# The second block's ssm input gathered with masked copies and matmuls, and the glu weight splits queued behind the last scan

## The chip, the cores and the metric

One core of a Trainium2 chip runs the whole program. The metric is the device time of one launch in microseconds (us). Engines are TensorE (PE; its weight loads are listed as PEld), VectorE (DVE), ScalarE (ACT), GpSimd (POOL) and SyncE (SP), which issues most transfers. Each engine runs its own instructions in order and waits on semaphores for the others.

## The reference, cut to what matters

The program is a trunk of two layers on a sequence of 256 steps with 1024 channels. Each layer is: half a SwiGLU feed-forward, a mixer, another half feed-forward, and a gated embedding, each with a normalization before and after. The first mixer is a differential attention, the second an S5 state-space layer followed by a GELU and a gated linear unit (glu). The change lies in the second mixer:

```
h = rmsnorm(x, g[2])
u = h in chunks, 64 groups of 16 channels, 64 complex states a group
state[t] = a * state[t-1] + B u[t]          (per group, complex, diagonal)
y[t] = Re(C state[t]) + d * u[t]
z = gelu(y) @ w_glu + b_glu
m = z[:, :1024] * sigmoid(z[:, 1024:])
```

## The kernel before, in words

The 256 steps are two blocks of 128 rows (b = 0, 1), held as x0 and x1 with a row per partition. Two generators (thread(0), thread(1)) walk the stages and share each weight tile; block 0 leads. Large matmuls are done in three passes: a weight tile is loaded raw by SP, ACT rounds it to a high part hi (line 129), VectorE subtracts to get the low part lo (line 131), and mm3 (lines 301 to 303) multiplies hi, lo and hi again. There are three raw buffers, so a new load waits until the lo of an earlier tile is done.

A planner orders the instructions of all engines from a model of their durations, except within ssm_core: there TensorE, VectorE and ACT keep the written order among the instructions of that function; instructions from outside it may still be put between them.

The ssm layer is computed by blocks of eight steps. Its input must be laid out so that a partition holds (step within eight, channel of the group) and the columns count groups and blocks of eight. ssm_u(b) (line 978) does the first half: as soon as a block's x is final, eight transfers per block copy x inside the on-chip memory into the tile ssmA, step s to slice s; those of block 0 go over SP's queue, those of block 1 over ACT's (six) and POOL's (two). ACT then squares the block (junku, line 1001), POOL makes the norm factor r, VectorE multiplies a 0/1 pattern with it (oh, line 1003). In ssm_core the order is: the embedding projection of both blocks (proj, 24 matmuls ppproj), two small matmuls that spread the norm factors (r_ps, line 1022), eight scaled copies ssmA to A2 (lines 1028 and 1030), then four gathers (lines 1050 to 1054: four transposes u_ps and one copy into ush each), mixed with the rest:

- chunk_states(pr): the states that each eight steps add, for a quarter of the groups (s_ps); needs the quarter of ush.
- turned(pr): transposes of them (st_ps). rotate(pr) and scan(pr) on VectorE: a rotation, two scans, a rotation back (lines 1092 to 1104); they give X.
- products(pr), outputs(pr): accumulate the direct part from ush and the part from X into y_ps. gated(hf): GELU on ACT, transposes y_tr, split into yT.
- glu_tile(n): lets one more glu weight tile be split (hi, lo); four such calls stand in the list. Other pending splits become free to go only after W.split_limit is raised at the end of ssm_core.

The glu matmuls (zglu) follow; the first 24 of each block need only the first half of yT and the first four weight tiles.

Of the kernel before, what the change touches and what calls it, by code (L numbers as in the profile page):

```python
# [140 lines left out]
def trunk(ctx, tc, x, p, norm_g, ffn_w_in, ffn_w_out, attn_w_qkv, attn_w_o, attn_lam, attn_subln_g,  # L141
# [835 lines left out]

    def ssm_u(b):

        if "A" not in ssm:  # L980
            gr = big_pool.tile([P, 640], F32, tag="hT_lo0", name="ssm_sel")
            ssm["R"], ssm["one"] = gr[:, 256:264], gr[:, 264:272]
            ssm["oh"], blk16 = [gr[:, 272:280], gr[:, 280:288]], gr[:, 288:304]
            ssm["sel"] = [gr[:, 320:448], gr[:, 448:576]]
            nc.vector.tensor_reduce(ssm["one"], ident.rearrange("p (j s) -> p s j", s=8), AX.X, ALU.add)
            nc.vector.tensor_reduce(blk16, ident.rearrange("p (j s) -> p j s", s=8), AX.X, ALU.add)
            for j in range(2):
                nc.gpsimd.memset(ssm["sel"][j], 0.0)
                nc.gpsimd.tensor_copy(ssm["sel"][j][:, 64 * j:64 * j + 64].rearrange("p (k q) -> p k q", q=4),
                                      blk16.rearrange("p (k o) -> p k o", o=1).broadcast_to([P, 16, 4]))  # L990
            ssm["A"] = big_pool.tile([P, 8, 256], F32, tag="hT_hi0", name="ssmA")
        xb = xs[b]
        steps_of = xb.rearrange("(k s) c -> s k c", s=8)
# [5 lines left out]
        junk = act_pool.tile([P, D], BF16, tag=f"xT_hi{b}", name=f"junku{b}")  # L999
        ss = small.tile([P, 1], F32, tag="ss", name=f"ssu{b}")  # L1000
        nc.scalar.activation(junk, xb, AF.Square, scale=1.0 / 32, accum_out=ss)
        r = rsqrt_of([ss], EPS, f"u{b}")
        nc.vector.tensor_scalar(ssm["oh"][b], ssm["one"], r, None, ALU.mult)
# [6 lines left out]
    def ssm_core(pool, pj, vs, tos, glu, heads):  # L1010

        A, v = ssm["A"], nc.vector
        W.split_limit = glu[0][0]
        both = [proj(b, 1, pj, heads[b]) for b in range(2)]
        for b in (0, 0, 0, 1, 1, 1):
            next(both[b], None)
        ush_xf = big_pool.tile([P, 2560], F32, tag="hT_hi1", name="ush")
        ush = ush_xf[:, :2048].rearrange("p (g t) -> p g t", t=P)
        A2 = big_pool.tile([P, 16, 8, 16], F32, tag="hT_lo1", name="ssmA2")
        rp = bank("a0", "r_ps")  # L1020
        for b in range(2):
            nc.tensor.matmul(rp[:, 0:8], ssm["sel"][b], ssm["oh"][b], start=b == 0, stop=b == 1)
        v.tensor_copy(ssm["R"], rp[:, 0:8])
        for s_ in range(8):
            dst = A2[:, :, 7 - s_, :]
            src = A[:, s_, :].rearrange("p (g h) -> p g h", h=16)
            if s_ % 3 == 2:
                nc.scalar.activation(dst, src, AF.Copy, scale=ssm["R"][:, s_:s_ + 1])
            else:
                v.tensor_scalar(dst, src, ssm["R"][:, s_:s_ + 1], None, ALU.mult)  # L1030
        S_xf = big_pool.tile([P, 2560], F32, tag="hT_lo0", name="ssmS")
        S = S_xf[:, :2048].rearrange("p (g r e n) -> p g r e n", g=8, r=2, e=2)
        xfs = [t[:, 2048:2560].rearrange("p (r c j) -> p r c j", r=2, j=32) for t in (S_xf, ush_xf)]
        yg = big_pool.tile([P, 2, 8, 8, 16], F32, tag="hT_hi0", name="ssmY")
        yT = [(act_pool.tile([P, KT, P], F32R, tag=f"xT_hi{b}", name=f"yThi{b}"),
               act_pool.tile([P, KT, P], F32R, tag=f"xT_lo{b}", name=f"yTlo{b}")) for b in range(2)]
        ssm["yT"] = yT
# [12 lines left out]
        def gather(g4, eng):  # L1050
            pt = ps_tr.tile([P, 512], F32, tag="tr", name=f"u_ps{g4}")
            for j in range(4):
                nc.tensor.transpose(pt[:, j * P:(j + 1) * P], A2[:, 4 * g4 + j].rearrange("p s h -> p (s h)"), ident)
            eng(ush[:, 4 * g4:4 * g4 + 4, :].rearrange("p a t -> p (a t)"), pt)

        def u_of(G):
            return ush[:, G].rearrange("p (m q) -> p q m", q=4)

        def chunk_states(pr):
            vv = ssm["V", pr] if pr < 2 else take2(vs[pr - 2])  # L1060
            for gg in range(2):
                gp = 2 * pr + gg
                acc = bank(f"a{gg}", f"s_ps{gp}")
                for e in range(2):
                    grouped(acc[:, e * P:(e + 1) * P], u_of(2 * gp + e), vv[gg][:, e * 512:e * 512 + 512],
                            start=True, stop=True)
                nc.scalar.copy(S[:, gp].rearrange("p r e n -> p e r n"),
                               acc[:, :2 * P].rearrange("p (e r n) -> p e r n", e=2, r=2))
# [9 lines left out]
        def rotate(pr):  # L1078
            er, rh = (ssm[k][:, 2 * pr:2 * pr + 2].rearrange("p g q j -> p (g q j)") for k in ("er", "rh"))
            er2 = er.rearrange("p (o x) -> p o x", o=1).broadcast_to([P, 2, 256])  # L1080
            eis = ssm["eis"][:, :, 2 * pr:2 * pr + 2].rearrange("p r g q j -> p r (g q j)")
            if pr % 2:
                r4 = big_pool.tile([P, 4, 2, 256], F32, tag="hT_lo1", name=f"rt{pr}")
# [12 lines left out]
        def scan(pr):  # L1096
# [7 lines left out]
            v.tensor_tensor(xf[:, :, :, 1:32], t1v[:, :, :, 0:31], t2v[:, :, :, 0:31], ALU.add)  # L1104
            X.append(xf.rearrange("p r c j -> p r (c j)"))

        def products(pr):
# [5 lines left out]
            for gg in range(2):  # L1113
                tt, to = take2(tos[2 * pr + gg])
                c0 = (2 * (pr % 2) + gg) * P
                for e in range(2):
                    grouped(accs_y[hf][e][:, c0:c0 + P], u_of(4 * pr + 2 * gg + e), tt[:, e * 512:e * 512 + 512],
# [32 lines left out]
        gather(0, nc.scalar.copy)  # L1150
        gather(1, v.tensor_copy)
        chunk_states(0)
        gather(2, nc.scalar.copy)
# [12 lines left out]
        scan(1)  # L1166
        turned(3)
# [12 lines left out]
        scan(3)  # L1180
# [3 lines left out]
        W.split_limit = len(specs)  # L1184

# [166 lines left out]
```

## Time and profile before

| | us |
|---|---|
| median of 3 runs (lowest, highest) | 1135.49 (1134.68, 1136.91) |
| the profiled execution, its own time | 1136.68 |
| its span, first to last instruction | 1134.9 |
| PE busy, share of the span | 1050.2, 93% |
| DVE busy, share | 690.1, 61% |
| ACT busy, share | 552.9, 49% |
| mean granted clock of TensorE (1 is full) | 0.967 |

A busy time sums an engine's instructions; overlapping ones count once. The ssm stage lies at about 811 to 880 us. In a list in order of time, a row gives the start, the length, the engine, the line, the operation, what it writes and reads, and how many alike it merges; in brackets how long the engine was idle before it and which instruction ended the wait. Two levels of TensorE's clock occur: 1.2 GHz (0.50) and 2.4 GHz (1.00).

### The profile page before, as it was taken

What the parts mean: (1) busy time and instruction counts of PE and PEld (TensorE: products, weight loads), DVE (VectorE), ACT (ScalarE), POOL (GpSimd) and SP (SyncE); (2) the same over time, 40 slices, a digit from 0 to 9 for tenths busy, and PEclk for the clock granted to TensorE, in tenths of its full rate; (3) what the DMA queues carried; (4) which work ended last, traced back from release to release, by engine and by line L of the source; (5) the groups of instructions that cost most, each with busy time, mean ns of one, the idle gap of its engine ahead of it and who ended that gap; (6) DMA issues with size and microseconds to landing.
All of it is one profiled execution on the core that took longest, in us unless ns stands there. A gap on an engine that the chain in (4) does not pass through costs nothing. (4 is left out here: it accounts for less than half of the span.)

```text
span 1134.9 us, 14522 instructions
## 1 busy us (share of the span) xinstructions
PE 1050.2 (93%) x5251; PEld 841.1 (74%) x5251; DVE 690.1 (61%) x1003; ACT 552.9 (49%) x872; POOL 241.7 (21%) x297
## 2 busy tenths in 40 slices
PE   6899999999998999998787998999776999999997
PEld 4688888788776887776565776888654878888885
DVE  6555554679558896555567563654357586555464
ACT  5544444566655544433464542553244475444354
POOL 6000000000020017878779412000100010000001
PEclk9899999999999999999898999999986999999999
DMA  7766556567447768566555669756874457665651
GB/s 225 225 185 186 185 189 193 161 201 219 146 96 192 222 187 219 187 203 211 161 169 165 182 176 335 237 178 220 285 256 149 154 164 231 183 193 163 210 168 56
DMA packets 119016, 217.58 MB, mean 192 GB/s; under 512 B 24832, under 2 KB 43168, under 8 KB 118944
## 3 DMA queue, kind: packets, MB, share of 16 engines
q1 hardware_dynamic: 115520, 210.14, 59.8%
q0 software_dynamic: 1888, 5.47, 2.0%
q10 hardware_dynamic: 1536, 1.05, 0.3%
q8 instruction: 41, 0.67, 0.3%
q14 instruction: 31, 0.25, 0.1%
HBM read 204.08 MB, written 15.69 MB: 194 GB/s over the span
## 5 line engine op out<-in xcount | busy, mean ns | idle before, releaser
L131 DVE TENSOR_TENSOR lo<-raw,hi 128x1024 fp32r<-128x1024 f32 x332 | 428.4, 1296 | 269.2 <-ACT hi L129 266.3
L129 ACT CAST hi<-raw 128x1024 fp32r<-128x1024 f32 x332 | 347.6, 1052 | 346.0 <-PE up L303 107.9
L301 PE MATMUL up<-hi,xThi 128*128 128x512 f32 x704 | 279.9, 401 | 13.0 <-ACT xThi L320 5.6
L302 PE MATMUL up<-lo,xThi 128*128 128x512 f32 x704 | 279.3, 398 | 2.1 <-DVE lo L131 2.0
L303 PE MATMUL up<-hi,xTlo 128*128 128x512 f32 x704 | 280.6, 404 | 0.0
L301 PEld LDWEIGHTS up<-hi,xThi 128*128 128x128 f32 x704 | 134.7, 192 | 42.3 <-ACT xThi L320 7.3
L302 PEld LDWEIGHTS up<-lo,xThi 128*128 128x128 f32 x704 | 134.7, 191 | 32.5 <-DVE lo L131 4.7
L303 PEld LDWEIGHTS up<-hi,xTlo 128*128 128x128 f32 x704 | 134.3, 192 | 29.1 <-issue 0.6
L301 PE MATMUL dn<-hi,hThi 128*128 128x512 f32 x352 | 139.9, 398 | 0.0
L302 PE MATMUL dn<-lo,hThi 128*128 128x512 f32 x352 | 139.0, 395 | 0.0
L303 PE MATMUL dn<-hi,hTlo 128*128 128x512 f32 x352 | 138.5, 394 | 0.0
L301 PEld LDWEIGHTS dn<-hi,hThi 128*128 128x128 f32 x352 | 67.0, 190 | 14.5 <-issue 0.8
L303 PEld LDWEIGHTS dn<-hi,hTlo 128*128 128x128 f32 x352 | 67.1, 191 | 14.2
L302 PEld LDWEIGHTS dn<-lo,hThi 128*128 128x128 f32 x352 | 67.1, 191 | 13.6
L312 POOL TENSOR_SCALAR v_pn<-sspn,sspn 128x1 f32<-128x1 f32 x8 | 3.4, 422 | 344.1 <-ACT junkpn L369 341.7
L320 ACT ACTIVATE xThi<-xT_ps,gT 128x128 fp32r<-128x128 f32 x112 | 38.6, 367 | 47.1 <-PE xT_ps L338 46.7
L325 DVE TENSOR_TENSOR hTlo<-hT_ps,hThi 128x512 fp32r<-128x512 f32 (+1 forms) x48 | 30.8, 644 | 40.3 <-ACT hThi L324 40.2
L324 ACT CAST hThi<-hT_ps 128x512 fp32r<-128x512 f32 (+1 forms) x48 | 26.4, 550 | 57.9 <-PE hT_ps L448 57.8
L321 DVE SCALAR_TENSOR_TENSOR xTlo<-xT_ps,gT,xThi 128x128 fp32r<-128x128 f32 x112 | 36.4, 345 | 23.8 <-ACT xThi L320 23.4
L338 PE MATMUL xT_ps<-ident,x 128*128 128x128 f32 x112 | 30.7, 298 | 16.0 <-DVE xTlo L321 11.1
L445 DVE SCALAR_TENSOR_TENSOR h<-up,r_pre,sg 128x512 f32<-128x512 f32 (+1 forms) x48 | 33.7, 702 | 15.7 <-ACT sg L443 10.5
L301 PE MATMUL qkvat<-hi,xThi 128*128 128x512 f32 x96 | 38.1, 397 | 0.2 <-ACT xThi L320 0.2
(342 smaller groups left out, 1281.9 us busy)
## 6 DMA issues: line engine op xcount, KB each, us to landing
raw<-in_ffn_w_in_dram SPq DMA_DIRECT2D x160, 512.0 KB, 4.3
raw<-in_ffn_w_out_dram SPq DMA_DIRECT2D x88, 512.0 KB, 4.1
raw<-in_attn_w_qkv_dram SPq DMA_DIRECT2D x24, 512.0 KB, 4.4
raw<-in_ffn_w_in_dram SPq DMA_DIRECT2D x32, 256.0 KB, 3.3
raw<-in_ple_w_gate_dram SPq DMA_DIRECT2D x16, 512.0 KB, 4.2
raw<-in_ssm_w_glu_dram SPq DMA_DIRECT2D x16, 512.0 KB, 3.3
gain<-in_norm_g_dram SPq DMA_DIRECT2D x8, 512.0 KB, 4.5
raw<-in_attn_w_o_dram SPq DMA_DIRECT2D x8, 512.0 KB, 4.3
```

What stands on the lines that cost most here:

```text
L129: nc.scalar.copy(hi, raw)
L131: (nc.gpsimd if n in self.on_pool else nc.vector).tensor_tensor(lo, raw, hi.bitcast(F32), ALU.subtract)
L301: nc.tensor.matmul(out_ap, st_hi, w_hi, start=start, stop=False)
L302: nc.tensor.matmul(out_ap, st_hi, w_lo, start=False, stop=False)
L303: nc.tensor.matmul(out_ap, st_lo, w_hi, start=False, stop=stop)
L312: nc.gpsimd.tensor_scalar(v, parts[0], parts[1], eps, ALU.add, ALU.add)
L320: return (nc.scalar.activation(hi, psum, AF.Copy, scale=scale).ins, nc.vector.scalar_tensor_tensor(lo, psum, scale, hi.bitcast(F32), ALU.m ...
L321: nc.vector.scalar_tensor_tensor(lo, psum, scale, hi.bitcast(F32), ALU.mult, ALU.subtract).ins)
L324: nc.scalar.copy(hi, psum)
L325: nc.vector.tensor_tensor(lo, psum, hi.bitcast(F32), ALU.subtract)
L338: marks[b].append(nc.tensor.transpose(pt, xb[:, k * P:(k + 1) * P], ident).ins)
L445: nc.vector.scalar_tensor_tensor(h[:, :w], up_, r, sg[:, :w], ALU.mult, ALU.mult)
```

## The change

Block 0's input keeps its transfers, but its r_ps matmul and scaled copies now lie in ssm_u, and its tiles hold 64 partitions. Block 1 has no transfers. For each quarter of the groups, masked(pr) copies x1 eight times, each time scaled with a 0/1 column (ssm "one") that keeps only the rows of one step, into a tile of weights; gather_second(pr) then multiplies 16 such 128x128 tiles with a 128x16 matrix rk (a 0/1 pattern times the norm factor), and gathered(pr) copies the result into ush. The order of ssm_core is rewritten: the first block's gathers come ahead of the projection, the second square stands in the list behind block 0's projection, one accumulator and one copy serve a chunk_states, rotate(2) comes ahead of the first gated, and some tiles change places. Last, W.hold gives every lo split that is traced after ssm_core a place behind the last instruction of scan(3) on VectorE's queue.

```diff
     def ssm_u(b):
-        if "A" not in ssm:
...
-        for s_ in range(8):
-            eng = nc.sync if b == 0 else nc.gpsimd if s_ % 3 == 2 else nc.scalar
-            eng.dma_start(ssm["A"][64 * b:64 * b + 64, s_, :], steps_of[s_].rearrange("k (q c) -> k q c", q=4))
         if b == 1:
             W.limit = len(specs)
+            return
...
+        A = big_pool.tile([64, 8, 256], F32, tag="hT_hi0", name="ssmA")
+        steps_of = xs[0].rearrange("(k s) c -> s k c", s=8)
+        for s_ in range(8):
+            nc.sync.dma_start(A[:, s_, :], steps_of[s_].rearrange("k (q c) -> k q c", q=4))
+        r = ssm_square(0)
+        nc.vector.tensor_scalar(oh, ssm["one"], r, None, ALU.mult)
+        rp = bank("a0", "r_ps")
+        nc.tensor.matmul(rp[0:64, 0:8], sel, oh, start=True, stop=True)
+        nc.vector.tensor_copy(R, rp[0:64, 0:8])
...
+        def gather_first(g4):
+            pt = ps_tr.tile([P, 512], F32, tag="tr", name=f"u_ps{g4}")
+            for j in range(4):
+                nc.tensor.transpose(pt[:, 64 * j:64 * j + 64], ssm["A2"][:, 4 * g4 + j].rearrange("p s h -> p (s h)"),
+                                    ident[0:64, 0:64])
+            nc.scalar.copy(ush5[:, 4 * g4:4 * g4 + 4, :, 0], pt[:, 0:256].rearrange("p (g k q) -> p g q k", g=4, q=4))
+        def masked(pr, tiles, engines):
+            per = 4 // len(tiles)
+            for s_ in range(8):
+                for n, t in enumerate(tiles):
+                    src = xs[1].rearrange("p (q r g h) -> p r q g h", q=4, r=4, g=4)[:, pr, per * n:per * n + per]
+                    dst = t[:, :, 7 - s_, :].rearrange("p (q g) h -> p q g h", g=4)
+                    if engines[s_] == "a":
+                        nc.scalar.activation(dst, src, AF.Copy, scale=ssm["one"][:, s_:s_ + 1])
+                    else:
+                        v.tensor_scalar(dst, src, ssm["one"][:, s_:s_ + 1], None, ALU.mult)
+        def gather_second(pr, tiles):
+            pt = bank("a1", f"u2_ps{pr}")
+            per = 16 // len(tiles)
+            for j in range(16):
+                nc.tensor.matmul(pt[:, 16 * j:16 * j + 16], tiles[j // per][:, j % per].rearrange("p s h -> p (s h)"),
+                                 ssm["rk"], start=True, stop=True, skip_group_check=True)
+            return pt
...
-        gather(0, nc.scalar.copy)
-        gather(1, v.tensor_copy)
+        for g4 in range(4):
+            gather_first(g4)
+        for _ in range(3):
+            next(both[0], None)
...
+        r1 = ssm_square(1)
+        masked(0, tiles[0], "vvvvvvvv")
+        v.tensor_scalar(ssm["rk"], ssm["blk"], r1, None, ALU.mult)
+        for _ in range(3):
+            next(both[1], None)
+        masked(1, tiles[1], "avavavav")
+        pt = gather_second(0, tiles[0])
+        gathered(0, pt, nc.scalar.copy)
         chunk_states(0)
+        masked(2, tiles[2], "avavavav")
+        pt = gather_second(1, tiles[1])
+        gathered(1, pt, v.tensor_copy)
+        tiles.append(big("hT_hi1", "m3"))
         turned(0)
+        masked(3, tiles[3], "avavavav")
+        rotate(0)
         chunk_states(1)
-        gather(3, nc.scalar.copy)
-        rotate(0)
+        pt = gather_second(2, tiles[2])
+        gathered(2, pt, nc.scalar.copy)
         scan(0)
         turned(1)
         chunk_states(2)
+        pt = gather_second(3, tiles[3])
+        gathered(3, pt, nc.scalar.copy)
         turned(2)
         chunk_states(3)
         products(0)
         products(1)
         rotate(1)
         scan(1)
+        outputs(0)
         turned(3)
-        outputs(0)
         products(2)
+        rotate(2)
         glu_tile(glu[0][0])
         outputs(1)
         gated(0)
-        rotate(2)
         glu_tile(glu[0][1])
         scan(2)
         products(3)
         glu_tile(glu[1][0])
         rotate(3)
         glu_tile(glu[1][1])
-        scan(3)
+        last = scan(3)
         outputs(2)
         outputs(3)
         gated(1)
         W.split_limit = len(specs)
+        W.hold = nullcontext, lambda: tc.issue_after(last.ins)
```

## Rows read from the trace of the kernel before

**Rows 1.** The page: its first line, the whole span.
```profile
span 1134.9 us, 14522 instructions
```

**Rows 2.** TensorE's matmuls in order of time through the stage: start, length, what, count.
```profile
816.73 0.28 PE L1022 MATMUL r_ps<-ssm_sel 128*128 128x8 f32 x2
827.15 0.60 PE L1022 MATMUL r_ps<-ssm_sel 128*128 128x8 f32 x2 [10.14 <-DVE ssm_sel L1003]
830.03 1.94 PE L1053 MATMUL u_ps<-ident,ssmA 128*128 128x128 f32 x8 [2.28 <-DVE ssmA L1030]
...
834.86 1.11 PE L1047 MATMUL s_ps<-V,ush 128*32 128x128 f32 x32
...
840.09 0.60 PE L1112 MATMUL y_ps<-zeros 1*128 1x512 bf16 x2
...
849.13 1.09 PE L1139 MATMUL y_tr<-ident,ssmY 128*128 128x128 f32 x8 [0.71 <-ACT ssmY L1134]
...
870.45 1.97 PE L1047 MATMUL y_ps<-lo,ush 64*32 64x128 f32 x64 [5.00 <-DVE ush L1104]
```

**Rows 3.** ACT in order of time; ACTq is the queue's issue of transfers.
```profile
813.57 1.23 ACT L484 COPY ppoproj<-ppproj 128x512 f32<-128x512 f32 x2 [1.40 <-POOL r_pn L316]
815.55 9.13 ACTq L996 DMA_DIRECT2D ssmA<-x  x6
824.73 1.06 ACT L1001 ACTIVATE junku<-x 128x1024 bf16<-128x1024 f32 x1 [9.93 <-DMA ssmA<-x]
...
833.19 0.37 ACT L1067 COPY ssmS<-s_ps 128x256 f32<-128x256 f32 x1 [1.45 <-PE s_ps L1047]
```

**Rows 4.** VectorE in order of time.
```profile
827.99 1.90 DVE L1030 TENSOR_SCALAR ssmA<-ssmA,ssm_sel 128x256 f32<-128x256 f32 x6
...
834.97 0.69 DVE L1092 TENSOR_TENSOR rthi<-st_ps,er 128x512 f32<-128x512 f32 x1 [2.27 <-PE st_ps L1075]
...
837.02 1.27 DVE L1099 TENSOR_TENSOR_SCAN rtlo<-rh,rtlo 128x256 f32<-128x256 f32 x2
...
840.31 0.68 DVE L1092 TENSOR_TENSOR rt<-st_ps,er 128x512 f32<-128x512 f32 x1
...
852.28 0.42 DVE L325 TENSOR_TENSOR yTlo<-y_tr,yThi 128x256 fp32r<-128x256 f32 x1 [0.44 <-ACT yThi L324]
...
861.97 2.35 DVE L131 TENSOR_TENSOR lo<-raw,hi 128x1024 fp32r<-128x1024 f32 x2
...
866.24 1.23 DVE L131 TENSOR_TENSOR lo<-raw,hi 128x1024 fp32r<-128x1024 f32 x1 [0.74 <-ACT hi L129]
...
868.59 1.22 DVE L131 TENSOR_TENSOR lo<-raw,hi 128x1024 fp32r<-128x1024 f32 x1
869.72 0.67 DVE L1104 TENSOR_TENSOR ush<-rt 128x496 f32<-128x496 f32 x1
```

**Rows 5.** Instructions on ssmA; durations in ns; landing of the last SP transfer alone.
```profile
L996 SPq DMA_DIRECT2D ssmA<-x x8: 529/592/607, 807.6 to 814.0; - x8
...
DMA to landing us min/median/max: 2.0/2.0/2.0
```

**Rows 6.** Stretches: length, busy time (instructions) by engine, granted clock, DMA share, GB/s.
```profile
811.00:817.00 6.00, 6.00 (x28) 4.91 (x27) 2.79 (x4) 2.36 (x6) 2.12 (x5) 1.00 0.76 199
817.00:827.00 10.00, 0.01 (x1) 0.00 (x0) 0.13 (x1) 2.11 (x4) 0.78 (x2) 0.67 1.03 375
830.00:834.20 4.20, 4.17 (x43) 3.39 (x44) 0.69 (x1) 1.25 (x3) 0.12 (x1) 0.53 1.02 405
854.40:858.20 3.80, 1.72 (x6) 0.86 (x5) 3.77 (x6) 0.69 (x1) 0.00 (x0) 0.95 0.35 116
870.40:878.60 8.20, 7.47 (x79) 5.77 (x80) 3.58 (x3) 3.21 (x5) 0.00 (x0) 0.52 0.57 192
```

**Rows 7.** TensorE's weight loads in order of time, two in a row after idle time.
```profile
313.58 0.19 PEld L301 LDWEIGHTS woat<-hi,oT_hi 128*128 128x128 f32 x1 [0.36 <-ACT oT_hi L320]
313.68 0.19 PEld L302 LDWEIGHTS woat<-lo,oT_hi 128*128 128x128 f32 x1
```

More of the change, by code (lines that the diff above doesn't have):

```diff
@@ L1001, in ssm_u @@
-        nc.scalar.activation(junk, xb, AF.Square, scale=1.0 / 32, accum_out=ss)
-        r = rsqrt_of([ss], EPS, f"u{b}")
-        nc.vector.tensor_scalar(ssm["oh"][b], ssm["one"], r, None, ALU.mult)
+            return
+        gr = const.tile([P, 128], F32, name="ssm_sel")
+        ssm["one"], ssm["blk"] = gr[:, 0:8], gr[:, 8:24]
+        oh, R, sel = gr[:, 24:32], gr[0:64, 32:40], gr[:, 64:128]
+        ssm["rk"] = gr[:, 40:56]
+        nc.vector.tensor_reduce(ssm["one"], ident.rearrange("p (j s) -> p s j", s=8), AX.X, ALU.add)
@@ L1010, in ssm_core @@
     def ssm_core(pool, pj, vs, tos, glu, heads):
-        A, v = ssm["A"], nc.vector
+        v = nc.vector
         W.split_limit = glu[0][0]
         both = [proj(b, 1, pj, heads[b]) for b in range(2)]
-        for b in (0, 0, 0, 1, 1, 1):
-            next(both[b], None)
-        ush_xf = big_pool.tile([P, 2560], F32, tag="hT_hi1", name="ush")
+        ush_xf = big_pool.tile([P, 2560], F32, tag="hT_hi0", name="ush")
         ush = ush_xf[:, :2048].rearrange("p (g t) -> p g t", t=P)
-        A2 = big_pool.tile([P, 16, 8, 16], F32, tag="hT_lo1", name="ssmA2")
@@ L1020, in ssm_core @@
[L1020 to L1030, printed above, removed]
@@ new lines, in masked @@
+        def masked(pr, tiles, engines):
+            per = 4 // len(tiles)
+            for s_ in range(8):
+                for n, t in enumerate(tiles):
[3 more added lines that the diff above has]
+                        nc.scalar.activation(dst, src, AF.Copy, scale=ssm["one"][:, s_:s_ + 1])
+                    else:
+                        v.tensor_scalar(dst, src, ssm["one"][:, s_:s_ + 1], None, ALU.mult)
@@ L1037, in ssm_core @@
-        ssm["yT"] = yT
         zeros = pool.tile([1, 512], BF16, tag="zeros", name="zeros", bufs=1)
@@ L1048, in grouped @@
                                  skip_group_check=True, **flags)
[L1050 to L1057, printed above, removed]
         def chunk_states(pr):
             vv = ssm["V", pr] if pr < 2 else take2(vs[pr - 2])
+            acc = bank("a0", f"s_ps{pr}")
             for gg in range(2):
-                gp = 2 * pr + gg
-                acc = bank(f"a{gg}", f"s_ps{gp}")
                 for e in range(2):
[L1065 to L1068, printed above, removed]
+                    grouped(acc[:, (2 * gg + e) * P:(2 * gg + e + 1) * P], ush[:, 4 * pr + 2 * gg + e, :].rearrange(
+                        "p (q m) -> p q m", q=4), vv[gg][:, e * 512:e * 512 + 512], start=True, stop=True)
+            nc.scalar.copy(S[:, 2 * pr:2 * pr + 2].rearrange("p g r e n -> p g e r n"),
+                           acc.rearrange("p (g e r n) -> p g e r n", g=2, e=2, r=2))
         def turned(pr):
@@ L1148, in glu_tile @@
             W.advance(n + NB)
-        gather(0, nc.scalar.copy)
-        gather(1, v.tensor_copy)
+        for g4 in range(4):
+            gather_first(g4)
+        for _ in range(3):
+            next(both[0], None)
+        tiles = [big("hT_hi1", "m0"), big("hT_lo0", "m1"),
+                 [act_pool.tile([P, 8, 8, 16], F32, tag=f"xT_{x}1", name=f"m2{x}") for x in ("hi", "lo")]]
+        r1 = ssm_square(1)
[6 more added lines that the diff above has]
+        gathered(0, pt, nc.scalar.copy)
         chunk_states(0)
-        gather(2, nc.scalar.copy)
+        masked(2, tiles[2], "avavavav")
+        pt = gather_second(1, tiles[1])
+        gathered(1, pt, v.tensor_copy)
+        tiles.append(big("hT_hi1", "m3"))
         turned(0)
+        masked(3, tiles[3], "avavavav")
+        rotate(0)
         chunk_states(1)
-        gather(3, nc.scalar.copy)
-        rotate(0)
+        pt = gather_second(2, tiles[2])
+        gathered(2, pt, nc.scalar.copy)
+        yg = big_pool.tile([P, 2, 8, 8, 16], F32, tag="hT_lo0", name="ssmY")
         scan(0)
@@ L1166, in ssm_core @@
         scan(1)
+        yT = [(act_pool.tile([P, KT, P], F32R, tag=f"xT_hi{b}", name=f"yThi{b}"),
+               act_pool.tile([P, KT, P], F32R, tag=f"xT_lo{b}", name=f"yTlo{b}")) for b in range(2)]
+        ssm["yT"] = yT
+        outputs(0)
         turned(3)
-        outputs(0)
         products(2)
+        rotate(2)
         glu_tile(glu[0][0])
```

45 lines of the change are left out of this document (23 added, 22 removed).

## The prediction

> **What bounds the kernel now.** All times are us from the start of the profiled span. The span is 1134.9 [rows 1]; the run's own time was 1136.68, so 1.8 lie around the span. The median of the runs shown is 1135.49, 1.2 under this execution. I sum against 1136.68 and take off 1.2 at the end. About 0.2% (2.3 us) is what a measurement of this kernel can tell from no change.
>
> I read the page first: TensorE is the busy engine, so only places where it idles or runs slowly can be won. Then TensorE's order of time around the ssm stage. Its matmuls are dense until the last projection matmul, about 816.7 [rows 2], and the reader is to see a hole of 10.1 before the second r_ps matmul at 827.15 and another of 2.3 before the gather transposes at 830.03 [rows 2]. The ACT order tells why: the second block's six transfers are issued on ACT's queue from 815.55 for 9.13, and the square, from which the block's norm factor comes, stands behind them in the same queue: it waited 9.9 and began at 824.73 [rows 3]. The second hole that matters is at the other end: the outputs at 870.45 wait 5.0 for the scan's last product [rows 2]. In the VectorE order that last product starts at 869.72, and among the operations of the last rotate and scan stand weight splits: two from 861.97, one at 866.24 (after 0.74 of waiting), one at 868.59 [rows 4]. One of these four belongs to the stage's own list (glu_tile), three were put in by the planner. From 870.45 on TensorE is nearly saturated, so a shift of that point goes to the end. The stage thus sets the time by when its gather may start, by TensorE's and VectorE's chain through it, and by TensorE's clock.
>
> **The start of the stage.** Removed: eight transfers of the second block, six of them with 9.13 of ACT's issue time. Added in their place on the path: the second square now stands (in the written order) behind the first block's gather and projection. TensorE's list now begins with gather_first, which needs the first block's transfers; these stay. The last was issued at 814.0 and landed 2.0 later [rows 5]: 816.0, and one scaled copy (0.32 on VectorE, rows 4; ACT, which takes every second one, somewhat longer) with its hand-over makes 816.6. So TensorE, which ran the 24 projection matmuls from about 811 on [rows 6], now idles from there to 816.6. The four groups of transposes are paced by their four ACT copies of 256 columns, 0.37 to 0.42 each [rows 3]: done by 818.7. Twelve projection matmuls take 2.6 at full clock (28 matmuls in 6.00, [rows 6]) and 5.2 at half; the clock will have fallen in the idle time, as it did after 817 [rows 6], so I take 4.7: 823.4. The last projection copy (half of 1.23, [rows 3]) ends at 824.2; from the square's start to the first matmul that uses its factor it was 2.42 before (824.73 to 827.15, rows 2 and 3). So rk is ready near 826.6. The masked copies of the first quarter, eight of 0.32 on VectorE (six took 1.90, [rows 4]), need only x, ready before its transfers were issued at 815.55 [rows 3]; they are hidden, with 5 us to spare. The gather thus starts at 826.6 against 830.03: 3.4 gained.
>
> **The gather itself.** Before: 16 transposes of 128 columns, eight of them in 1.94 at the low clock [rows 2]. After: for the second block 64 matmuls with 128x128 weights and 16 moving columns. The trace shows each plain float matmul as two passes with a weight load each (two r_ps matmuls are four instructions), so one quarter is 16 matmuls, 32 passes. No row has 32 such passes in a run, so I bound one. From below: the columns alone are short, and the tiled y_ps passes, whose weights are 32 wide, follow each other at 64 in 1.97 at half clock, 0.031 [rows 2]. From above: two weight loads of 128 columns in a row stand 0.10 apart at full clock (313.58 and 313.68, [rows 7]); the r_ps pair, with only 8 moving columns, takes 0.28 from its first start to its last end at full clock and 0.60 at half [rows 2], 0.14 and 0.30 a pass with the run-out in it. The r_ps rows are the nearest by far (same weights, nearly the same columns), so I stay between the 0.10 of the loads and these 0.14: 0.11 a pass at full clock, 3.5 a quarter, 14.0 for four; twice that, 0.22 and 7.0 a quarter, at half.
>
> TensorE then goes, at full clock: 826.6, four quarters 14.0, four chunk_states at 1.11 [rows 2] 4.4, four waits of 0.7 in which a quarter is copied out before its chunk_states may start (0.4 copy and the hand-overs; the turned transposes lie in these waits) 2.8: 847.8. From the zero matmuls to the first y_tr transposes it was 840.09 to 849.13 before [rows 2], 9.0, and this work is the same, only reordered: y_tr at 856.8 against 849.13, 7.7 later. So TensorE's added weight loads, which are on the path since every chunk_states waits for its quarter, eat the 3.4 and 7.7 more. VectorE keeps up: its rotate and scan pair takes 5.3 (834.97 to 840.31, [rows 4]), and after the start at about 837.5 two of them and the third rotate end near 850, before y_tr.
>
> **The end of the stage.** Before, VectorE finished the y splits at 852.70 (852.28 and 0.42), 3.6 after y_tr began, and then needed 17.7 to 870.39 [rows 4]. After, the third rotate (2.0) is already done in the time in which VectorE waits, and the three outside splits with their wait (3 x 1.13 and 0.74, 4.1) come behind the scan. What is left behind the y splits is three splits of the stage's own 3.4, scan 3.3, rotate 2.0, scan 3.3: 12.0. So 856.8 + 3.6 + 12.0 = 872.4 for the scan's end against 870.39: 2.0 later. The moved splits cost nothing there: TensorE has the second block's matmuls on the first four tiles to run before it needs them. If that cover were gone, three splits would cost 3.4. Their raw buffers come free later as well, so SP's weight loads slip by some 5 us; 24 matmuls at 0.22 to 0.43, 5 to 10, cover it. One thing is given back: before, TensorE came out of its 5.0 hole at half clock, 0.52 granted over 870.4 to 878.6 [rows 6], which cost up to half of the 7.47 busy there, 3.5. After, the outputs and tiles lie closer together, and none to all of this may be saved. At full clock in the gather the change is thus +2.0 less 0 to 3.5, about +0.3.
>
> **The clock in the gather decides.** The clock fell to the 1.2 GHz level after the idle time behind 817, and again by 858.2 after a stretch in which TensorE had only six matmuls (1.72 busy of 3.80), and rose after 4.17 busy of 4.20 with 128-column work [rows 6]. From 826.6 to 848 TensorE would spend two thirds of its time loading weights and streaming 16 columns at a time. No row shows what the clock does in such a stretch; I take it to be nearer to the stretch before 858.2, where TensorE did little, than to the dense 128-column work before the rise. If it falls after the first quarter: the second quarter 3.5 more and its chunk_states 1.1 for sure; the third and fourth quarter with theirs and the products (2 x 4.6 and 2.4, 11.6) at half or back at full, take half, 5.8. Together 10.4 on top of 0.3: +10.7; TensorE's chain stays the bound, so all of it shows. With the fall later or earlier by one quarter: +5 to +17.
>
> **The rivals.**
> A, the forecast: the clock falls in the gather: 1136.68 + 10.7 = 1147.4, in the median 1146.2; own range 1140 to 1153. For it: the fall behind the sparse stretch before 858.2. Against: B's reason.
> B: the clock holds. +0.3, median 1135.8, own range 1132.5 to 1139. For it: TensorE is never idle for long in the gather, while both falls in rows 6 follow idle time.
> C, the other side: the weight loads overlap far better than the r_ps pair shows, and a pass costs about 0.03. A quarter is then 1.0, TensorE's chain shortens by 10, and VectorE binds: rotate from about 833, two pairs 10.7, rotate and split 3.1, y_tr by then at 847, splits to 851, 12.0: 863 to 865, 6 earlier, median 1129.5; with some of it lost to the clock 1131. It decides below 0.08 a pass. Against it: rows 2 and 7.
> The Trainium skill speaks for C on one page: "TensorE: Matmul & The Clock Gate", section "Back-to-back issue gap", puts matmuls of 1 to 64 columns at a floor of about 25 ns each, by which a quarter would be an estimated 0.8. Its section on LDWEIGHTS makes a load cost by its columns, about 107 ns for 128, with no fast load for FP32; the r_ps rows agree with the second.
> That the splits' order doesn't take effect would put 4.1 back on A, B or C; I see nothing in the code that would undo it and give it no chance of its own.
>
> **How the numbers follow.** A 0.45, B 0.35, C 0.20. All of A is slower. B around +0.3 gives faster 0.07, same 0.16, slower 0.12. C is faster but for 0.01 or so. Faster 0.26, same 0.17, slower 0.57. The range goes from 1130.5, which leaves out half of C, to 1152, which leaves out a tenth of A's top.
>
> **What would show it.** In the profile after: no transfers on ACT's queue; gather start near 826.6 (a start after 829 would say that the first block's gather or projection is the late one); the spacing of the 32 passes (0.11, 0.22 or 0.03); the granted clock from 827 to 860; y_tr near 857 (B), 865 or later (A), 847 (C); no outside split between the last rotate and the last product; that product's end against 870.39. I am wrong if the passes are much shorter than the r_ps pair's, or the clock stays up and the tail gains more than 2.

## The result, and the profile after

The changed kernel took 1151.37 us in the median (1148.35 to 1157.46, 6 runs) against 1136.08 (1132.96 to 1141.23, 6 runs) of the kernel before on the same chip: ratio 1.0143, 95% interval 1.0105 to 1.0182 (the quotient of the two medians is 1.0135). It is slower, in the way of case A, and by more than A's 1146.2. The profiled execution took 1157.46, the longest of the six and 6.1 over their median; its mean granted clock was 0.958.

```profile
span 1155.7 us, 14803 instructions
```

TensorE in order of time through the stage (as [rows 2]). The first row, dn, is the last matmul ahead of the stage; y_ps<-zeros are the zero matmuls with which the products begin, called "the zeros" below; the last row is that of the last outputs:

```profile
810.70 0.39 PE L303 MATMUL dn<-hi,hTlo 128*128 128x512 f32 x1
...
818.04 2.30 PE L1033 MATMUL u_ps<-ident,ssmA 64*128 64x64 f32 x16 [6.74 <-ACT ssmA L1011]
...
827.41 4.98 PE L1054 MATMUL u_ps<-ssm_sel,m 128*128 128x16 f32 x32 [0.22 <-DVE ssm_sel L1178]
832.89 1.93 PE L1076 MATMUL s_ps<-V,ush 128*32 128x128 f32 x32 [0.51 <-issue]
...
834.75 7.01 PE L1054 MATMUL u_ps<-ssm_sel,m 128*128 128x16 f32 x32
...
854.23 7.01 PE L1054 MATMUL u_ps<-ssm_sel,m 128*128 128x16 f32 x32
...
863.92 0.60 PE L1131 MATMUL y_ps<-zeros 1*128 1x512 bf16 x2
864.45 1.96 PE L1076 MATMUL y_ps<-hi,ush 128*32 128x128 f32 x64
...
873.16 1.17 PE L1159 MATMUL y_tr<-ident,ssmY 128*128 128x128 f32 x8 [2.45 <-ACT ssmY L1154]
...
889.18 1.96 PE L1076 MATMUL y_ps<-lo,ush 64*32 64x128 f32 x64 [1.79 <-DVE ush L1124]
```

The four quarters of the gather are the x32 rows: the first took 4.98, the others 7.01 (the third stands as two rows of 16, not shown). The windows over the four quarters (length, busy time and count of PE, PEld, DVE, ACT, POOL, granted clock, DMA share, GB/s) say why:

```profile
827.40:832.40 5.00, 4.98 (x32) 4.87 (x32) 2.56 (x12) 2.01 (x5) 0.00 (x0) 0.73 0.98 365
834.70:841.80 7.10, 7.10 (x37) 7.05 (x34) 0.00 (x0) 4.52 (x13) 0.00 (x0) 0.50 0.43 148
844.40:851.60 7.20, 7.20 (x38) 7.11 (x35) 4.00 (x7) 0.65 (x2) 0.00 (x0) 0.50 0.00 0
854.20:861.30 7.10, 7.10 (x37) 7.07 (x34) 0.00 (x0) 0.61 (x2) 0.00 (x0) 0.50 0.45 150
```

The clock fell in the first quarter (0.73 in the mean of its window) and was at 1.2 GHz (0.50) in the windows of the other three, while PE was listed as busy without a gap and its weight loads nearly so. Behind the zeros it was full again: the 64 passes at 864.45 took 1.96, as in e1 below.

The two profiled spans, cut at the same events, give the whole difference of 20.8. In the left column are the start times before and after; "predicted" is what the prediction's terms make of the same stretch.

| stretch | before | after | difference | predicted |
|---|---|---|---|---|
| to the gather's start (830.03, 827.41) | 830.03 | 827.41 | -2.6 | -3.4 |
| gather to zeros (840.09, 863.92) | 10.06 | 36.51 | +26.5 | +20.3 |
| zeros to y_tr (849.13, 873.16) | 9.04 | 9.24 | +0.2 | +1.2 |
| y_tr to the last outputs (870.45, 889.18) | 21.32 | 16.02 | -5.3 | -5.7 |
| last outputs to the end | 264.45 | 266.52 | +2.1 | -1.7 |
| sum | | | +20.8 | +10.7 |

(The 1.2 is the half of the 2.4 that the prediction wrote for the products, which stand behind the zeros.) Two lines hold nearly all of the error: the gather, 6.2 too low, and the tail, 3.8 too low. The tail's first 43 to 45 us, up to the last glu matmul, show in the windows of the kernel before and then of the changed one:

```profile
870.45:913.20 42.75, 41.75 (x232) 33.77 (x232) 24.98 (x30) 19.43 (x26) 1.53 (x2) 0.91 0.52 161
```

```profile
889.18:933.90 44.72, 42.38 (x231) 34.08 (x231) 28.39 (x33) 21.50 (x28) 1.52 (x2) 0.90 0.56 177
```

The same matmuls, 2.0 longer: 2.3 idle in place of 1.0, and 0.6 more busy. Most of the 0.6 is the clock, which rose somewhat later behind the outputs: the second y_tr took 1.44 in place of 1.04. These rows, of the kernel before, are its second y_tr and the first yTlo behind it:

```profile
878.36 1.04 PE L1139 MATMUL y_tr<-ident,ssmY 128*128 128x128 f32 x8
```

```profile
880.78 0.42 DVE L325 TENSOR_TENSOR yTlo<-y_tr,yThi 128x256 fp32r<-128x256 f32 x1
```

The 1.3 more of idle time are one wait of TensorE in the changed kernel, the second row here:

```profile
897.12 1.44 PE L1159 MATMUL y_tr<-ident,ssmY 128*128 128x128 f32 x8
...
902.66 0.50 PE L301 MATMUL zglu<-hi,yThi 128*128 128x512 f32 x1 [1.29 <-ACT yThi L324]
```

VectorE and ACT of the changed kernel show where this wait comes from:

```profile
889.04 3.49 DVE L131 TENSOR_TENSOR lo<-raw,hi 128x1024 fp32r<-128x1024 f32 x3
...
897.27 2.60 DVE L131 TENSOR_TENSOR lo<-raw,hi 128x1024 fp32r<-128x1024 f32 x2 [1.37 <-ACT hi L129]
900.37 1.23 DVE L131 TENSOR_TENSOR lo<-raw,hi 128x1024 fp32r<-128x1024 f32 x1 [0.50 <-ACT hi L129]
901.51 0.42 DVE L325 TENSOR_TENSOR yTlo<-y_tr,yThi 128x256 fp32r<-128x256 f32 x1
```

```profile
893.60 1.05 ACT L129 CAST hi<-raw 128x1024 fp32r<-128x1024 f32 x1 [1.82 <-DMA raw<-in_ssm_w_glu_dram]
894.55 0.59 ACT L1154 ACTIVATE ssmY<-y_ps 128x512 f32<-128x512 f32 x1
```

The three moved splits come at 889.04, so their raw buffers come free and are loaded again later. ACT's next rounding then waits 1.82 for its load, with the second half of the gelu (894.55) behind it in the queue; and three later splits stand ahead of yTlo, for which ACT's next yThi waits in turn. From the second y_tr (897.12) to the first yTlo it was 4.4, and 2.4 in the kernel before.

Two cautions hold for all start times and for the tail. The last dn matmul, ahead of every edit, begins anywhere from 805.36 (e8) to 812.70 (e10) in the traces of this document, so start times of two traces are best counted from it. And the stretch from the last outputs to the end took 264.7 to 267.8 in the other traces with the line of W.hold as in the change (e1, e3, e4, e5, e8 to e11), and 264.3 to 265.5 in the three without it (before, e2, e6): the tail's +2.1 is one value out of such a spread.

### The profile page after: what moved, and what is told of

Read it like the earlier page. It is cut to its first block, busy times and chain, and to the rows that moved or that the text cites. A ratio compares the mean times of both kernels' runs of the same rounds, so it can differ in the third digit from the quotient of the medians.

```text
span 1155.7 us, 14803 instructions
## 1 busy us (share of the span) xinstructions
PE 1074.7 (93%) x5377; PEld 865.8 (75%) x5377; DVE 694.7 (60%) x1025; ACT 559.5 (48%) x890; POOL 241.6 (21%) x292
## 5 line engine op out<-in xcount | busy, mean ns | idle before, releaser
L303 PEld LDWEIGHTS dn<-hi,hTlo 128*128 128x128 f32 x352 | 66.8, 190 | 14.3
L301 PEld LDWEIGHTS dn<-hi,hThi 128*128 128x128 f32 x352 | 66.7, 190 | 14.3 <-issue 0.8
L445 DVE SCALAR_TENSOR_TENSOR h<-up,r_pre,sg 128x512 f32<-128x512 f32 (+1 forms) x48 | 33.6, 702 | 14.3 <-ACT sg L443 9.4
```

Of the source, the lines that this page charges most:

```text
L301: nc.tensor.matmul(out_ap, st_hi, w_hi, start=start, stop=False)
L303: nc.tensor.matmul(out_ap, st_lo, w_hi, start=False, stop=stop)
L445: nc.vector.scalar_tensor_tensor(h[:, :w], up_, r, sg[:, :w], ALU.mult, ALU.mult)
```

## The experiments

Each was timed together with runs of the kernel before on one chip: e1 to e4 on one, e5 to e8 on a second, e9 to e11 on a third. The ratios, with 95% intervals, are to those; their medians lie within 0.8 us of each other, which is to be kept in mind where two rows of the table are compared.

| run | median us (runs) | ratio to the kernel before |
|---|---|---|
| e1_wide | 1138.46 (12) | 1.0014, 0.9990 to 1.0038 |
| e2_nohold | 1155.99 (6) | 1.0176, 1.0135 to 1.0216 |
| e3_hold | 1137.03 (12) | 1.0002, 0.9977 to 1.0028 |
| e4_projfirst | 1148.83 (6) | 1.0106, 1.0064 to 1.0148 |
| e5_both | 1132.38 (12) | 0.9975, 0.9950 to 0.9999 |
| e6_both_nohold | 1135.33 (12) | 1.0006, 0.9985 to 1.0027 |
| e7_both_order | 1138.12 (12) | 1.0021, 1.0001 to 1.0041 |
| e8_twice | 1150.06 (6) | 1.0133, 1.0100 to 1.0166 |
| e9_wide64 | 1138.36 (10) | 1.0037, 1.0016 to 1.0058 |
| e10_wide32 | 1153.10 (4) | 1.0166, 1.0122 to 1.0211 |
| e11_both64 | 1140.36 (7) | 1.0037, 1.0016 to 1.0059 |

**Is it the clock, or the passes themselves? (e1_wide)** Each matmul of the gather moves 128 columns in place of 16, the added ones zeros that the later matmuls overwrite or that nothing reads: more work for TensorE. For this rk gets a tile of its own and one memset; e10 below has both too, with 32 columns, and is not faster than the changed kernel.

```diff
-        ssm["rk"] = gr[:, 40:56]
+        ssm["rk"] = const.tile([P, 128], F32, name="ssm_rk")
+        nc.gpsimd.memset(ssm["rk"], 0.0)
...
-                nc.tensor.matmul(pt[:, 16 * j:16 * j + 16], ...
+                nc.tensor.matmul(pt[:, 16 * j:16 * j + 128], ...
...
-        v.tensor_scalar(ssm["rk"], ssm["blk"], r1, None, ALU.mult)
+        v.tensor_scalar(ssm["rk"][:, 0:16], ssm["blk"], r1, None, ALU.mult)
```

> The changed kernel with 128 instead of 16 moving columns in each of the 64 gather matmuls (rk padded with zeros; the surplus columns are overwritten by the next matmul or never read). Number of passes and weight loads unchanged, eight times the columns. Theory (the low clock is the cost, and it falls because TensorE streams little between weight loads): the granted clock stays at 1.00 from about 829 to 864, a quarter of 32 passes takes 3.5 to 3.9 us instead of 7.0, y_tr starts near 857 to 860, the time falls by 10 to 17 us to 1135 to 1141. Rival (weight loads of 128 columns cost 0.22 us here for themselves, and the columns only add): a quarter stays at 7 us or grows, time 1151 or more.

TensorE's rows, then the window over the second quarter:

```profile
824.63 3.84 PE L1055 MATMUL u_ps<-ssm_rk,m 128*128 128x128 f32 x32 [0.22 <-DVE ssm_rk L1179]
...
845.98 0.60 PE L1132 MATMUL y_ps<-zeros 1*128 1x512 bf16 x2
...
871.72 1.16 PE L1077 MATMUL y_ps<-lo,ush 64*32 64x128 f32 x64 [1.81 <-DVE ush L1125]
...
876.41 1.03 PE L1160 MATMUL y_tr<-ident,ssmY 128*128 128x128 f32 x8
```

```profile
830.00:833.80 3.80, 3.80 (x38) 3.80 (x35) 0.00 (x0) 3.68 (x12) 0.00 (x0) 1.00 0.77 296
```

Eight times the columns, and 12.9 less in the median: the clock holds at 1.00, a quarter takes 3.84 in place of 7.01, and the gather to the zeros 21.35 in place of 36.51. That is case B's path to within a fraction of a us (21.2 predicted) and its end to within 3 (1135.8 predicted). The low clock is 13 of the 15 us that the change costs.

**How much of TensorE's own work shows at the end? (e8_twice)** The wide run with every second-block gather done twice into the same place.

```diff
-            for j in range(16):
+            for j in (*range(16), *range(16)):
```

> The wide run with each gather_second done twice into the same place, so 4 x 3.84 = 15.4 more of TensorE's work at full clock and nothing else. Theory (every chunk_states waits for its quarter, so TensorE's chain through the gather sets the end): all of it shows, 1138.5 + 15.4 = 1153.8. Rival (VectorE's chain of rotates and scans binds beside it, with room for part): 1146 to 1150, with the wait of rotate for its states unchanged for some quarters.

```profile
821.29 7.41 PE L1055 MATMUL u_ps<-ssm_rk,m 128*128 128x128 f32 x64 [0.20 <-DVE ssm_rk L1179]
...
856.93 0.60 PE L1132 MATMUL y_ps<-zeros 1*128 1x512 bf16 x2
```

A further quarter costs 3.57 (7.41 less 3.84), 14.3 for four; the gather to the zeros took 35.64, which is 14.3 more, and the median rose by 11.6. 1150.06 lies under the 1153.8 expected and at the top of the rival's 1146 to 1150. The path to the zeros took all of the 14.3, so TensorE's chain binds there, not VectorE's. Where 2.7 of it went in the median is not settled; the interval (3.8 to either side) covers that much, and in the traces the stretch from the zeros to the end was 290.1 here and 292.1 in e1.

**What the moved splits are worth (e2_nohold, e3_hold).** The last line of the change taken out of the changed kernel, and put alone into the kernel before (there scan also returns its last instruction, as in the change).

```diff
 e2: the changed kernel
-        W.hold = nullcontext, lambda: tc.issue_after(last.ins)
 e3: the kernel before
...
-        scan(3)
+        last = scan(3)
...
+        W.hold = nullcontext, lambda: tc.issue_after(last.ins)
```

> The changed kernel without its last line, so that the outside weight splits may again go between the operations of the last rotate and scan. Theory (the splits' order shortens VectorE's end by the 4.1 us that three splits and a wait take, less what is given back behind it): last product 3 to 4 us later, time 1 to 4 us longer than the changed kernel, 1152 to 1155. Rival (the splits' delay behind the scan gives all of it back, through later y splits): within 1 us of the changed kernel.

> The kernel before with the second edit alone: the outside splits are queued behind the last product of scan 3. Theory: the last product ends near 866.3 instead of 870.4, 4.1 us earlier, of which 2 to 4 reach the end: 1132 to 1134. Rival (given back later): 1135 to 1137, no change that can be measured.

VectorE in e2, from y_tr (867.70) on, with outside splits among the last rotate and scan again:

```profile
879.23 2.35 DVE L131 TENSOR_TENSOR lo<-raw,hi 128x1024 fp32r<-128x1024 f32 x2
...
882.75 1.23 DVE L131 TENSOR_TENSOR lo<-raw,hi 128x1024 fp32r<-128x1024 f32 x1
...
885.09 1.22 DVE L131 TENSOR_TENSOR lo<-raw,hi 128x1024 fp32r<-128x1024 f32 x1
886.23 0.67 DVE L1124 TENSOR_TENSOR ush<-rt 128x496 f32<-128x496 f32 x1
```

From y_tr to the end of the last product it was 19.2 in e2 and 15.97 with the line, 3.2 less. The medians differ by 4.6, but more than half of either interval lies in the other, so the line's worth there is not clear of noise. In the kernel before, the line took the y_tr-to-outputs stretch from 21.32 [rows 2] to 17.3 and gave nothing at the end. There the gain turns into a wait of ACT's queue, shown by ACT and then TensorE of e3:

```profile
873.57 1.05 ACT L129 CAST hi<-raw 128x1024 fp32r<-128x1024 f32 x1 [3.29 <-DMA raw<-in_ssm_w_glu_dram]
874.52 0.59 ACT L1134 ACTIVATE ssmY<-y_ps 128x512 f32<-128x512 f32 x1
```

```profile
869.11 1.16 PE L1047 MATMUL y_ps<-lo,ush 64*32 64x128 f32 x64 [1.81 <-DVE ush L1105]
875.17 0.80 PE L301 MATMUL zglu<-hi,yThi 128*128 128x512 f32 x1 [4.90 <-ACT ssmY L1134]
```

The outputs no longer wait 5.0 for the last product [rows 2]; a rounding whose load is late stands ahead of the gelu, and TensorE waits 4.90 for that.

**Can the start come earlier? (e4_projfirst)** In the changed kernel the first block's gather waits for its transfers (6.74 at 818.04) with the projection behind it. Here the second square and both projections come first.

```diff
-        for g4 in range(4):
-            gather_first(g4)
-        for _ in range(3):
-            next(both[0], None)
...
         r1 = ssm_square(1)
+        for i in (0, 0, 0, 1, 1, 1):
+            next(both[i], None)
...
-        for _ in range(3):
-            next(both[1], None)
+        for g4 in range(4):
+            gather_first(g4)
```

> The changed kernel with block 1's square and both projections ahead of the first block's gather in the written order, all else the same. Theory (the start is set by the order: first block's transfers, then its gather, then the projection, then the square): the 64 gather matmuls start near 819 to 820 instead of 827.4, the clock still falls in the gather, a quarter still takes 7 us, time 6 to 8 us less than the changed kernel, 1143 to 1146. Rival (the start doesn't count, the chain behind it does): less than 2 us.

```profile
815.62 7.01 PE L1054 MATMUL u_ps<-ssm_sel,m 128*128 128x16 f32 x32
...
854.22 1.03 PE L1131 MATMUL y_ps<-zeros 1*128 1x512 bf16 x2
855.18 3.64 PE L1076 MATMUL y_ps<-hi,ush 128*32 128x128 f32 x64
```

The gather starts 11.8 earlier than in the changed kernel, but 4.5 of this lie ahead of the stage: the last dn matmul began at 806.15 here and at 810.70 there. Counted from it, the gather starts 7.2 earlier (9.5 behind it in place of 16.7), the zeros 5.2 and the last outputs 2.5 (75.9 behind it in place of 78.5). The rest went to the clock: all four quarters ran at the low one (38.60 from start to zeros, against 36.51), and so did the products (3.64 for 64 passes, against 1.96). The median gained 2.5 too, short of the 6 to 8 expected, and the intervals of the two overlap. A start alone did not pay while the gather ran at half speed.

**Both together (e5_both), and how the line of W.hold stands then (e6_both_nohold, e7_both_order).** e5 is e4 with e1's rk. e6 is e5 without W.hold. e7 is e5 with the outside work held back further: roundings behind the second gelu, splits behind the last y split.

```diff
 e7 against e5
...
-        W.hold = nullcontext, lambda: tc.issue_after(last.ins)
+        W.hold = (lambda: tc.issue_after(gelu.ins)), lambda: tc.issue_after(ylo.ins)
```

> The changed kernel with the 128-column rk of the wide run and the written order of the projection-first run. Theory (the gather costs what TensorE's clock makes of it, and its start is set by what stands ahead of it): both gains add. In the projection-first run the gather started at 815.6; in the wide run it was 21.35 from the gather's start to the zeros (824.63 to 845.98) and 9.2 from there to y_tr: zeros at 837, y_tr at 846.2, last product near 863, 9.0 earlier than in the wide run, so 1138.5 - 9.0 = 1129.5. If the first quarter still runs at the half clock after the idle time ahead of it, 3.8 more: 1133. Rival (the wide run's time is already held by VectorE's chain or by the weight loads behind the stage): the start comes 9 earlier and the outputs do, but the time stays at 1136 to 1138. Rival (the clock falls at the start of the gather and stays down as in the projection-first run, whatever the columns): quarters at twice 3.84, about 1146.

> The same as the run with both, without the W.hold line. Theory (the moved splits take 4 to 5 off the scan's chain and give about 2 back before the second y splits): 2 to 4 slower than the run with both, and outside splits stand again among the last rotate and scan. Rival (the gain is given back whole at full clock, as in the kernel before with W.hold alone, which was 0.3 from the kernel before): within 1.5 of it.

> The same as the run with both, but the outside roundings (hi) stand behind the second gelu on ACT and the outside splits (lo) behind the last y split on VectorE, in place of behind the last product. Theory (splits ahead of yTlo and roundings between the two gelus delay the second half of y by 2 to 4, for which TensorE waits): y_tr(1) follows the outputs by 2 to 4 less, and the time is 2 to 3 under the run with both, about 1127. Rival (the raw buffers come free later, so the weight tiles come later and TensorE waits for them in the glu): the same time or up to 5 slower, with TensorE's waits on hi or lo in zglu.

TensorE of e5, then the first quarter of e6 alone:

```profile
815.58 3.84 PE L1055 MATMUL u_ps<-ssm_rk,m 128*128 128x128 f32 x32
...
836.92 0.60 PE L1132 MATMUL y_ps<-zeros 1*128 1x512 bf16 x2
...
846.17 1.09 PE L1160 MATMUL y_tr<-ident,ssmY 128*128 128x128 f32 x8 [2.45 <-ACT ssmY L1155]
...
862.19 1.80 PE L1077 MATMUL y_ps<-lo,ush 64*32 64x128 f32 x64 [1.80 <-DVE ush L1125]
```

```profile
815.91 5.47 PE L1055 MATMUL u_ps<-ssm_rk,m 128*128 128x128 f32 x32
```

e5 met its path to 0.9 (zeros at 837, y_tr at 846.2, last product near 863 expected), in part by luck: its last dn matmul began at 806.28, as early as that of e4, from which the start was taken. At 1132.38 it is 6.1 under e1 of the nine expected, and just under the kernel before: the interval ends at 0.9999. The nine were differences of start times in two traces, and 2.5 of them lie ahead of the stage (dn at 808.69 in e1, at 806.15 in e4). Counted from dn, e5's gather starts 6.6 earlier than e1's (9.3 behind it in place of 15.9), and that is what the medians show. The profiled execution of e5 (1128.73) is 3.7 under its median; its first quarter ran at full clock, while those of e6 and e7, whose code differs only behind it, took 5.47, with the clock low for a part. So a low clock in the first quarter, which the expectation also allowed for, may be part of e5's median; this is not shown.

e6 is 3.0 over e5, as the theory had it (from y_tr to the end of the last product 19.6 in place of 16.0), though the intervals overlap a little. e7 is slower than e5: there the theory on the order behind the scan fell. VectorE of e7 waits for the y split with the held work behind it:

```profile
875.39 0.42 DVE L325 TENSOR_TENSOR yTlo<-y_tr,yThi 128x256 fp32r<-128x256 f32 x1 [8.45 <-ACT yThi L324]
```

TensorE put its second y_tr no sooner after the outputs (7.36, against 7.44 in e5), and 8.45 of VectorE's time went unused. In the 43 us behind the outputs TensorE was busy 39.88 in e7 and 41.51 in e5; in e7 it waited there for yThi (1.16 and 0.19) and for a split (1.09), in e5 for one split (0.76). That is 1.6 of the 5.6 by which the stretch from the outputs to the end is longer in e7's trace; the rest lies later and is not explained.

**How wide must the matmuls be here? (e9_wide64, e10_wide32, e11_both64)** e9 and e10 are e1 with 64 and 32 columns, e11 is e5 with 64.

```diff
-        ssm["rk"] = const.tile([P, 128], F32, name="ssm_rk")
+        ssm["rk"] = const.tile([P, 64], F32, name="ssm_rk")
...
-                nc.tensor.matmul(pt[:, 16 * j:16 * j + 128], ...
+                nc.tensor.matmul(pt[:, 16 * j:16 * j + 64], ...
```

> The wide run with rk of 64 columns in place of 128. A pass is bounded by its weights, not its columns, so at full clock a quarter is 3.5 to 3.84, as at 16 and at 128. Theory (the clock falls by how little of a pass is columns): 64 columns are half of the 128 and four times the 16, nearer to the 128 of the run in which the clock held: it holds, quarters near 3.6, 1138. Rival (half the columns are not enough): quarters of 7.0 from the second on as in the changed kernel, 1150. Between (it falls in part of the gather): 1142 to 1147.

> The wide run with rk of 32 columns. Theory as for 64: 32 are nearer to the 16 of the changed kernel, the clock falls during the gather, quarters of 7.0 from the second on, 1149 to 1152. Rival: it holds at 32 too, quarters near 3.5, 1138, and then only the narrowest columns lower it.

> The run with both (wide rk, projection first), with 64 columns. Theory: if the clock holds at 64 columns, quarters of 3.5 to 3.6 in place of 3.84, so up to 1.2 under the run with both (1132.4): 1131 to 1132.4. Rival (the clock doesn't hold from the start of the gather, since TensorE has just been idle): as in the projection-first run, 1144 to 1149.

In e9 all quarters took 3.79 at a clock of 1.00, and the time is e1's. e10 took 1153.10; in its profiled execution the clock fell at the end of the second quarter and rose and fell again in the next two:

```profile
832.97 3.76 PE L1055 MATMUL u_ps<-ssm_rk,m 128*128 128x32 f32 x32
837.49 1.94 PE L1077 MATMUL s_ps<-V,ush 128*32 128x128 f32 x32
839.36 2.31 PE L1055 MATMUL u_ps<-ssm_rk,m2hi 128*128 128x32 f32 x16
...
845.99 4.19 PE L1055 MATMUL u_ps<-ssm_rk,m 128*128 128x32 f32 x32
```

The quarters of 7.0 that were expected from the second on are not in this trace: the later two took some 4.2. From the gather to y_tr it lost 5.7 against e1 (36.29 in place of 30.59); the rest of the 10.2 between the two traces lies ahead of the stage (dn 4.0 later) and in the tail. That execution (1150.14) was the shortest of e10's four, with a mean granted clock of 0.964; the others had 0.958, 0.951 and 0.964, so the time came as expected, but its way there is shown only in part. e11 shows a gather that begins at the low clock, after TensorE had been half idle (1.69 busy of the 3.5 before the gather, at 0.83 granted):

```profile
818.56 7.09 PE L1055 MATMUL u_ps<-ssm_rk,m 128*128 128x64 f32 x32
...
828.02 7.09 PE L1055 MATMUL u_ps<-ssm_rk,m 128*128 128x64 f32 x32
...
843.02 3.79 PE L1055 MATMUL u_ps<-ssm_rk,m 128*128 128x64 f32 x32
```

Two quarters at the low clock, two at the full one: 64 columns kept the clock where it was full at the start (e9), but it came back late where it was not, and e11's median is 8.0 over e5's (the gather to the zeros took 29.72 in place of 21.34). Ahead of e5's gather TensorE was as idle (1.39 busy of 3.0), yet the clock was still at 1.00 there; e6 and e7, with 128 columns, met the low clock in the first quarter and were out of it before the second. These are single executions. What the chip asks for to raise or keep the clock is not worked out from these runs.

## Why the prediction was right or wrong

**Start: right in size, its last digit by luck.** 827.41 against 826.6. Counted from the last dn matmul, the gather starts 16.7 behind it here and 15.0 to 16.4 in the five other traces with this order, against 19.0 before (811.06 to 830.03): 2.3 to 4.0 gained, 3.4 written. The transposes of the first block came at 818.04, 1.4 later than written, behind ACT's scaled copies; the projection behind them took back a part.

**The pass: right.** 0.22 at half clock (7.01 for 32), as bounded by the loads and the r_ps pair [rows 2, 7]. At full clock 3.76 to 3.84 were measured, with 32 to 128 columns; with 16 no quarter ran at full clock throughout, but in e2 half a quarter did, 16 passes in 1.96 (granted 1.00 in 844.97 to 846.70), as long as in e1 with 128 columns (1.95 and 2.05). Case C, with passes of 0.03, is refuted:

```profile
844.97 1.96 PE L1054 MATMUL u_ps<-ssm_sel,m2hi 128*128 128x16 f32 x16
```

On the floor of about 25 ns for 1 to 64 columns ("TensorE: Matmul & The Clock Gate", section "Back-to-back issue gap", of the Trainium skill) the measurement decides: the 32 further passes of a quarter in e8 took 3.57, 112 ns each, with new 128-column float weights for each; the page's section "LDWEIGHTS (loading the stationary operand)", an estimated 107 ns for 128 columns, is the one that describes this gather at full clock.

**The path at full clock: right.** 21.2 from the gather's start to the zeros, 21.35 in e1 and 21.34 in e5; y_tr to the last product 15.6, 15.97 measured. The rotate moved ahead and the splits moved behind did what the prediction counted on.

**The clock's fall: the mechanism right, the term too small.** This is the step that failed: "take half, 5.8" of the 11.6 of the third and fourth quarter and the products. In the trace the clock did not come back in the gather; second, third and fourth quarter all ran at half, and the first in part, while the products, for which 2.4 of the 11.6 were written, ran at full clock. Against e1 the low clock cost 15.2 in the profiled execution (36.51 less 21.35), 12.9 in the medians, against 10.4 predicted. That the clock would fall at all was right on a ground that the trace does not bear out: the prediction likened the gather to a stretch in which TensorE did little (1.72 busy of 3.80), and called it against A that TensorE would never be idle for long. The windows of the changed kernel show the clock at 0.50 in stretches where PE is listed as busy 7.10 of 7.10: being listed as busy did not keep it up. Why it falls there is not shown; e1 shows that more columns undo it.

**The tail: wrong in sign.** "0 to 3.5 may be saved" because TensorE would come to the outputs at full clock. In the changed kernel it came to them at half clock again (1.96 for 64 passes, as before), behind its waits for VectorE's splits and scans. In e1 they ran at full clock (1.16), and the saving was there at first: the second y_tr came 4.7 behind the outputs, in place of 7.9 before. But the first yTlo came 10.9 behind them (882.59), 10.3 before, and the stretch from the outputs to the end was still 266.4 against 264.45. So what the clock gave was spent on waiting: the prediction left out that later weight loads, late roundings and a late second half of y would set this stretch, as the rows of VectorE and ACT show. "The moved splits cost nothing" holds for the matmuls on the four first tiles, which the prediction looked at, and not for the y splits and the gelu queued behind the outside work, which it did not.

**The net of the splits.** 4.1 was the price written for them; e2 puts it at 4.6 in the changed kernel, which is not clear of noise, e6 at 3.0 at full clock, and e3 at nothing in the kernel before. The prediction took 0.2% for what can be told from no change; with 4 to 12 runs the intervals here are 0.2 to 0.4% to either side.

**What stays open.** The profiled execution lies 6.1 above the median. The two executions of 1157 had a mean granted clock of 0.958 and 0.955, the four of 1148 to 1152 had 0.961 to 0.965. An estimate from these: a mean clock lower by 0.007 over 1150 us is 8 us of work at full clock, and 7 divide the two groups. So the clock can account for the difference. That the shorter executions had a part of the gather at full clock would fit e2, whose profile shows quarters of 4.50 and 3.98 beside 7.01; where in the program they were faster is not shown, since only one execution was traced.

## What to carry to other kernels

Before trading transfers for many narrow matmuls, price them at TensorE's low clock as well as at the full one: matmuls whose time is the loading of new float weights can let the clock fall while TensorE looks fully busy, and then what stands between them on the path runs at half speed too (here a chunk_states, 1.93 at 832.89). If the loads bind anyway, a wider moving operand is nearly free, and here it was worth 13 us with 64 or 128 columns, and nothing with 32. And when work is moved behind a critical instruction, list what stands behind it in its new place: each of the queues (VectorE, ACT, the buffers that it frees) passes the delay on.

## What the runs showed of the hardware that was not expected

- More work made the kernel faster: eight times the columns in the gather, 1151.37 to 1138.46, with the granted clock in the second quarter at 1.00 in place of 0.50.
- The columns cost next to nothing: at full clock a quarter took 3.76, 3.79 and 3.84 at 32, 64 and 128 columns, and half a quarter 1.96 at 16.
- TensorE's clock stayed at 1.2 GHz in the gather's windows from 834.7 to 861.3, with 7.10 busy of 7.10. The Trainium skill lists 1.2 GHz as the state of an idle array ("TensorE: Matmul & The Clock Gate", section "Part 1: The HAM clock gate (the "warmup" mystery)"); here the row decides: an array that the profile lists as busy without a gap had that clock too.
